# Down projections by Strassen–Winograd products on pairs of row blocks, with the first two row blocks of each half computed by themselves from the same operands

## The chip, the cores and the metric

One core of a Trainium2 chip runs the whole program. The metric is the device time of one execution in microseconds (us). TensorE (PE) does the matmuls and loads their weights on a second track (PEld), VectorE (DVE), ScalarE (ACT) and GpSimd (POOL) work on the data in SBUF and PSUM, and SyncE (SP) issues the loads of the weights.

## The reference

Two layers, an S5 mixer and a differential attention, each followed by a gated MLP with a convolution of width 3. The change concerns the last line of `conv_ffn`, the product with `w_down`.

```python
D_MODEL, SEQ, D_FF = 1024, 512, 2816

def conv_ffn(h, w_up, conv_w, conv_b, w_down):
    u = h @ w_up
    ...
    g, val = jnp.split(u, 2, axis=-1)
    return (jax.nn.silu(g) * val) @ w_down

def reference(x, ...):
    h = x
    for i in range(DEPTH):
        hn = rmsnorm(h, norm_mix_g[i])
        ...
        h = h + conv_ffn(rmsnorm(h, norm_ffn_g[i]), ffn_w_up[i], ...)
    return rmsnorm(h, final_norm_g)
```

## The kernel before

Everything is held transposed: 128 features on the partitions, 512 positions along a row. `h` has 8 row blocks (1024 features), the hidden layer of the MLP has 22 (2816).

**Numbers.** A float32 operand is split into hi (rounded to fp32r by an ACT copy) and lo (the rest, by a DVE subtraction). A product of two 128-blocks is three matmuls, hi by hi, hi by lo and lo by hi (`mm3`, L801 to L804). The third of them is the first that needs the lo of the weights.

**Weights.** `WStream` (L112 to L150) brings one unit after another from DRAM into `raw` (two buffers, transfers issued by SP) and splits it into hi (L139, ACT) and lo (L141, DVE, a few by POOL). A unit of an up projection has 2048 columns, split in halves of 1024. A unit of a down projection has 1408 columns, 11 blocks of 128 for one row block of the result, split in a first part of 640 columns (blocks k = 0 to 4) and a second part of 768 (k = 5 to 10). The hi and lo tiles have two buffers of 2048 columns. The next unit is split while the present one is multiplied.

**The MLP** (`ffn`, L909). `up(j)` computes for the hidden block j the two groups gv = 0 (gate) and gv = 1 (value) of 24 matmuls of 512 columns. When a group ends, `evac` (L918) multiplies it by the norm on DVE (`tpb`, L927) and `conv` (L933) runs one group later: two STT (scalar_tensor_tensor) of the convolution (L934, L935), SiLU or the product of the two (L944), and the hi (ACT, L945) and lo (DVE, L946) of the result, which is an operand of the down projection. `up` runs for j = 0 to 11, `down(0)` takes blocks 0 to 10 (half 0), `up` runs for j = 12 to 21, `down(1)` takes blocks 11 to 21 (half 1). In `down` (L993), each row block m is one PSUM bank of 11 × 3 matmuls of 512 columns, added into `h[:, m]` on DVE (L1005). In half 1 the norm of the next stage is begun with each row block (`norm_part`, L815): a square on ACT, a sum into `ssum` on POOL (L829), in layer 0 also the hi and lo (`xlo`, L821) of the next stage's input. In layer 1 the last two row blocks are done by `finish` in halves of 256 columns.

**Order.** Each engine runs its instructions in the order in which the program is written out; a semaphore holds an instruction back until what it reads is there. The second part of a unit's lo, and what `conv` leaves behind, are written out behind the `tpb` of the last group, so at the start of `down` DVE still has that queue to work through.

Stages, by the trace: S5 mixer and its gate to 211 us, layer 0 up 211 to 345, down half 0 to 407, up to 519, down half 1 to 581, attention to 859, layer 1 up to 993, down half 0 to 1055, up to 1167, down half 1 and the finish to the end.

Of the kernel before, what the change touches and what calls it, by code (L numbers as in the profile page):

```python
# [37 lines left out]
def trunk(ctx, tc, xs, xt, sp, bx, cx, sv, vec, lamv, biasw, wglu, wup, wdn, wv, wqk, wo, out):  # L38
# [72 lines left out]

    class WStream:  # L112
# [11 lines left out]

        def split(self, half, parts="hl", eng=V):

            i = self.ns
            if i >= len(units):
                return
            n = units[i][1]  # L130
            if half == 0 and "h" in parts:
                self.hl[i] = (
                    self.whl.tile([128, 2048], F32R, tag="hi", name=f"hi{i}"),
                    self.whl.tile([128, 2048], F32R, tag="lo", name=f"lo{i}"),
                )
            h0, h1 = (0, n // 256 * 128) if half == 0 else (n // 256 * 128, n)
            hi, lo = self.hl[i]
            if "h" in parts:
                S.activation(hi[:, h0:h1], self.raw[i][:, h0:h1], AF.Copy)  # L139
            if "l" in parts:  # L140
                eng.tensor_tensor(lo[:, h0:h1], self.raw[i][:, h0:h1], hi[:, h0:h1].bitcast(F32), op=ALU.subtract)  # L141
                if half == 1:
                    del self.raw[i]
                    self.ns += 1

        def start(self):
            self.cur += 1
            while self.nd < min(self.cur + 3, len(units)):
                self.dma()
            return self.hl.pop(self.cur)  # L150
# [573 lines left out]
    ws.whl = pool("whl", 2, "right")  # L724
# [71 lines left out]
    xhi = xnp.tile([128, 8, 512], F32R, name="xhi")  # L796
# [18 lines left out]
    def norm_part(m, gcol, first, split=True):  # L815

        settle()
        if split:
            gc = vect[:, gcol + m:gcol + m + 1]
            S.activation(xhi[:, m], h[:, m], AF.Copy, scale=gc)  # L820
            pend.append(lambda: V.scalar_tensor_tensor(  # L821
                xlo[:, m], h[:, m], gc, xhi[:, m].bitcast(F32), op0=ALU.mult, op1=ALU.subtract))
# [86 lines left out]
    def ffn(l, next_gcol):  # L909
        fp = pool(f"ffn{l}", 1, "left")  # L910
        tpb = [fp.tile([128, 514], F32, name=f"tpb{i}") for i in range(4)]
# [3 lines left out]
        acts = {}  # L915
        state = {"rb": None, "slot": None, "nt": 0}
# [4 lines left out]
        def evac(j, gv, ps):  # L921
            tb = tpb[state["nt"] % 4]
# [5 lines left out]
            acc = fp.tile([128, 512], F32, tag="acc", name="acc", bufs=4)  # L928
# [4 lines left out]
        def conv(j, gv, tb, cw, acc):  # L933
# [7 lines left out]
            if j % 4 == 0:  # L941
                state["slot"] = arena(F32R, [128, 4, 2, 512], f"act{l}_{j}")
            hi, lo = (state["slot"][:, j % 4, i] for i in range(2))
            V.tensor_tensor(a0, a0, acc, op=ALU.mult)  # L944
            S.activation(hi, a0, AF.Copy)  # L945
            later.append(lambda: V.tensor_tensor(lo, a0, hi.bitcast(F32), op=ALU.subtract))  # L946
            acts[j] = (hi, lo)
# [44 lines left out]

        def down(hf):  # L993
            flush()
            for m in range(8 if hf == 0 or l == 0 else 6):
# [5 lines left out]
                ps = psd[0].tile([128, 512], F32, tag="mm", name="ps", bufs=6)  # L1001
# [3 lines left out]
                V.tensor_tensor(h[:, m], ps, h[:, m], op=ALU.add)  # L1005
                if hf == 1 and l == 0:
                    norm_part(m, next_gcol, m == 0)
                elif hf == 1:
                    norm_part(m, next_gcol, m == 0, False)
                    S.activation(hg[:, m], h[:, m], AF.Copy, scale=vect[:, next_gcol + m:next_gcol + m + 1])  # L1010

        def finish():
# [36 lines left out]
            for c in range(2):  # L1049
                cs = slice(256 * c, 256 * c + 256)  # L1050
                for m in (6, 7):
# [7 lines left out]
                    ps = psd[0].tile([128, 512], F32, tag="mm", name="ps", bufs=6)[:, 0:256]  # L1059
                    for k in range(11):  # L1060
                        ah, al = acts[11 + k]
                        mm3(ps, wh[:, k * 128:k * 128 + 128], wl[:, k * 128:k * 128 + 128], ah[:, cs], al[:, cs],
                            k == 0, k == 10)
# [6 lines left out]
                    V.tensor_tensor(h[:, m, cs], ps, h[:, m, cs], op=ALU.add)  # L1070
# [11 lines left out]
        for j in range(12, 22):  # L1082
            up(j)
        down(1)
# [16 lines left out]
    for eh in range(2):  # L1101
        vps = [bank(t, "vps") for t in (("sc", "sc", "sc", "tr"), ("pj", "pj", "pv", "sc"))[eh]]
        for un in range(4):
            wh, wl = ws.start()
            ws.split(0)
            ws.split(1)
            for kl in range(2):
# [289 lines left out]
    fin = pool("fin", 1, "left")  # L1397
    hg = fin.tile([128, 8, 512], F32, name="hg")
# [4 lines left out]
    fin.release()  # L1403
# [108 lines left out]
```

## Time and profile before

| | us |
|---|---|
| median of 3 runs (1245.04 to 1246.16) | 1245.08 |
| the profiled execution | 1244.49 |
| its span, first to last instruction | 1242.7 |
| PE busy | 1181.4 (95%) |
| DVE busy | 826.3 (66%) |
| ACT busy | 583.3 (47%) |
| POOL busy | 253.1 (20%) |

The mean granted TensorE clock is 0.981. The page gives busy times and the chain of work that ended last. The timeline gives each instruction its start, its duration and, in brackets, the idle time of its engine before it and what ended that. Neighbouring instructions overlap in their records, so the spacing of starts is what an instruction takes of its engine in a row of like ones. In the windows view the granted clock is 1.00 at 2.4 GHz and 0.50 at 1.2 GHz.

### The profile page before, as it was taken

How to read it: one execution, taken by the hardware profiler on the slowest of the kernel's cores; microseconds unless marked ns; L12 is line 12 of the kernel's file. 1: busy time of each engine (PE TensorE's matmuls, PEld its weight loads, DVE VectorE, ACT ScalarE, POOL GpSimd, SP SyncE). 2: the span in 40 equal slices, each digit the busy share in tenths (PEclk: the TensorE clock that was granted, in tenths of full speed). 3: DMA queues.
4: the chain of work that ended last, by engine and by line, in shares of the span. 5: the costliest groups of instructions: out<-in, count | busy, mean ns of one | idle time of the engine just before them, and what ended most of it. 6: DMA issues, size and time to landing. Idle time of an engine off the chain costs nothing.

```text
span 1242.7 us, 16642 instructions
## 1 busy us (share of the span) xinstructions
PE 1181.4 (95%) x6402; PEld 933.9 (75%) x6402; DVE 826.3 (66%) x1654; ACT 583.3 (47%) x1008; POOL 253.1 (20%) x271
## 2 busy tenths in 40 slices
PE   3886899999999999999999999999999999999996
PEld 1663688888878888788876777678888878888786
DVE  8999866667653476744349899977767643566634
ACT  6775654444422344433247777655444421344431
POOL 3999424000000000011033434423000000000011
PEclk8998899999999999999999999999999999999998
DMA  5005323123233122132332323221222233122222
GB/s 219 2 3 136 137 74 104 66 102 102 81 102 109 69 98 102 70 117 71 98 107 83 90 75 108 70 76 63 96 77 94 81 117 125 68 96 75 92 94 68
DMA packets 23391, 112.32 MB, mean 90 GB/s; under 512 B 2704, under 2 KB 5392, under 8 KB 16144
## 3 DMA queue, kind: packets, MB, share of 16 engines
q1 hardware_dynamic: 21472, 108.64, 25.7%
q0 software_dynamic: 1280, 2.10, 0.9%
q8 instruction: 50, 0.82, 0.3%
q10 hardware_dynamic: 560, 0.52, 0.1%
q14 instruction: 29, 0.24, 0.1%
HBM read 102.86 MB, written 2.10 MB: 84 GB/s over the span
## 4 chain that ended last, share of the span: by engine, by line
PE 84%; DVE 5%; issue 1%; DMA 0%; ACT 0%; DVEq 0%; ACTq 0%
PE ps L803 20%; PE ps L804 20%; PE ps L802 20%; PE pj L802 2%; PE pj L804 2%; PE pj L803 2%; PE po L802 1%; PE po L803 1%; PE po L804 1%; PE vps L1112 1%; PE vps L1114 1%; PE vps L1113 1%; DVE qkt L1165 1%; PE ptp L1266 1%; PE sc L1231 1%; PE sc L1234 1%
## 5 line engine op out<-in xcount | busy, mean ns | idle before, releaser
L802 PE MATMUL ps<-xhi,hi 128*128 128x512 f32 x672 | 266.6, 397 | 0.0
L804 PE MATMUL ps<-xhi,lo 128*128 128x512 f32 x672 | 265.4, 395 | 0.0
L803 PE MATMUL ps<-xlo,hi 128*128 128x512 f32 x672 | 265.0, 394 | 0.0
L139 ACT ACTIVATE hi<-raw 128x1024 fp32r<-128x1024 f32 (+2 forms) x216 | 184.1, 874 | 113.6 <-PE ps L803 85.9
L141 DVE TENSOR_TENSOR lo<-raw,hi 128x1024 fp32r<-128x1024 f32 (+3 forms) x178 | 188.3, 1077 | 43.5 <-ACT hi L139 41.8
L927 DVE TENSOR_TENSOR tpb<-ps,rb 128x512 f32<-128x512 f32 x88 | 60.8, 693 | 149.7 <-PE ps L804 144.5
L929 ACT ACTIVATE acc<-tpb,vect 128x512 f32<-128x512 f32 x88 | 71.6, 816 | 168.1 <-DVE tpb L927 168.1
L804 PEld LDWEIGHTS ps<-xhi,lo 128*128 128x128 f32 x672 | 126.2, 188 | 31.1
L803 PEld LDWEIGHTS ps<-xlo,hi 128*128 128x128 f32 x672 | 126.2, 188 | 30.4
L802 PEld LDWEIGHTS ps<-xhi,hi 128*128 128x128 f32 x672 | 126.2, 188 | 30.0
L803 PE MATMUL ps<-act,hi 128*128 128x512 f32 (+1 forms) x374 | 143.2, 383 | 0.2
L802 PE MATMUL ps<-act,hi 128*128 128x512 f32 (+1 forms) x374 | 143.1, 383 | 0.0
L804 PE MATMUL ps<-act,lo 128*128 128x512 f32 (+1 forms) x374 | 142.9, 382 | 0.0
L827 POOL COPY ssum<-sqt 128x512 f32<-128x512 f32 x4 | 2.5, 626 | 656.2 <-ACT sqt L824 656.2
L1005 DVE TENSOR_TENSOR h<-ps,h 128x512 f32<-128x512 f32 x30 | 20.7, 691 | 107.5 <-PE ps L804 107.5
L141 POOL TENSOR_TENSOR lo<-raw,hi 128x512 fp32r<-128x512 f32 (+1 forms) x38 | 61.2, 1616 | 125.4 <-ACT hi L139 125.3
L803 PEld LDWEIGHTS ps<-act,hi 128*128 128x128 f32 x374 | 70.3, 188 | 16.0 <-DVE act L946 1.1
L804 PEld LDWEIGHTS ps<-act,lo 128*128 128x128 f32 x374 | 70.2, 188 | 16.1 <-DVE lo L141 1.4
L802 PEld LDWEIGHTS ps<-act,hi 128*128 128x128 f32 x374 | 70.3, 188 | 14.9
L935 DVE SCALAR_TENSOR_TENSOR acc<-tpb,vect,acc 128x512 f32<-128x512 f32 x88 | 66.2, 752 | 3.1
L934 DVE SCALAR_TENSOR_TENSOR acc<-tpb,vect,acc 128x512 f32<-128x512 f32 x88 | 65.5, 745 | 0.6 <-ACT acc L929 0.6
L945 ACT ACTIVATE act<-acc 128x512 fp32r<-128x512 f32 x44 | 27.9, 634 | 66.2 <-DVE acc L944 66.2
(262 smaller groups left out, 2048.7 us busy)
## 6 DMA issues: line engine op xcount, KB each, us to landing
raw<-wup SPq DMA_DIRECT2D x44, 1024.0 KB, 4.8
raw<-wdn SPq DMA_DIRECT2D x32, 704.0 KB, 4.0
raw<-wqk SPq DMA_DIRECT2D x16, 512.0 KB, 3.5
raw<-wglu SPq DMA_DIRECT2D x4, 1024.0 KB, 4.8
raw<-wv SPq DMA_DIRECT2D x8, 512.0 KB, 3.5
raw<-wo SPq DMA_DIRECT2D x4, 1024.0 KB, 4.9
bias<-biasw SPq DMA_DIRECT2D x8, 448.0 KB, 4.2
cxt<-cx SPq DMA_DIRECT2D x1, 2064.0 KB, 15.8
```

The costliest lines, as they stand in the source:

```text
L139: S.activation(hi[:, h0:h1], self.raw[i][:, h0:h1], AF.Copy)
L141: eng.tensor_tensor(lo[:, h0:h1], self.raw[i][:, h0:h1], hi[:, h0:h1].bitcast(F32), op=ALU.subtract)
L802: PE.matmul(ps, lhsT=wh, rhs=xh, start=first, stop=False)
L803: PE.matmul(ps, lhsT=wh, rhs=xl, start=False, stop=False)
L804: PE.matmul(ps, lhsT=wl, rhs=xh, start=False, stop=last)
L927: V.tensor_tensor(tb[:, 1:513], ps, state["rb"], op=ALU.mult)
L929: S.activation(acc, tb[:, 1:513], AF.Identity, bias=cb, scale=cw[1])
L934: V.scalar_tensor_tensor(acc, tb[:, 0:512], cw[0], acc, op0=ALU.mult, op1=ALU.add)
L935: V.scalar_tensor_tensor(acc, tb[:, 2:514], cw[2], acc, op0=ALU.mult, op1=ALU.add)
L945: S.activation(hi, a0, AF.Copy)
L1005: V.tensor_tensor(h[:, m], ps, h[:, m], op=ALU.add)
L1112: PE.matmul(vps[q], lhsT=xh, rhs=wk_h, start=(k == 0), stop=False)
```

## The change

Row blocks 2 to 7 of each down projection are computed in pairs (m, m+1). For each kp = 0 to 4 the two row blocks, two hidden blocks (2kp and 2kp+1) and two halves of 256 positions make a 2 × 2 by 2 × 2 product of blocks, for which Winograd's form of Strassen's algorithm takes seven block products in place of eight. A pair has 7 × 5 × 3 matmuls of 256 columns, and 2 × 2 × 3 for the eleventh hidden block ("left"), 117 in all, where two row blocks before had 66 of 512. `finish` still does row blocks 6 and 7 of layer 1's second half, so there are 3 + 3 + 3 + 2 = 11 pairs.

The operands of the activations are 7 tiles of 256 columns (`Acts`): op 0 is made when the even hidden block is done (`first`), the other six when the odd one is (`second`, with four DVE sums of 256 columns, and a lo of 1024 columns one group later). The weights' sums are made in `down` on DVE (`Pair.total`, 640 columns each), partly in the raw buffers themselves. In half 1, kp = 0 is put off by one group. A tile's hi and lo come from a pool of four buffers of 1024 columns, and a raw buffer's next transfer is issued where its last reader is written out, not in `start`. `tpb` and `acc` have three buffers in place of four, and `xlo` of row blocks 2 to 7 in layer 0 is made in the stage after. Rows 0 and 1 use the same operands: the even hidden blocks' first halves go to a bank `p1` (15 matmuls of 256 columns), then the odd blocks (15 of 512), then 15 of 256 with the difference (op 3), then left (3 of 512): 30 of 256 and 18 of 512 where there were 33 of 512.

```diff
+    class Pair:
...
+        def total(self, n):
+            w = self.view
+            if n == 2:
+                V.tensor_tensor(w(1), w(1, 0), w(1, 1), op=ALU.add)
+            elif n == 3:
+                V.tensor_tensor(w(1), w(1), w(0, 0), op=ALU.subtract)
+            elif n == 4:
+                self.x = self.ws.xtile().rearrange("p (n k c) -> p n k c", n=2, c=128)
+                V.tensor_tensor(self.x[:, 0], w(0, 1), w(1), op=ALU.subtract)
+            else:
+                V.tensor_tensor(self.x[:, 1], w(0, 0), w(1, 0), op=ALU.subtract)
...
+        def done(self, r):
+            del self.ws.raw[self.i + r]
+            self.ws.dma()
...
+        def tiles(self):
+            return [self.whl.tile([128, 1024], F32R, tag=t, name=t) for t in ("hi", "lo")]
...
-    ws.whl = pool("whl", 2, "right")
+    ws.whl = pool("whl", 4, "right")
...
+            wait = hf == 1 and kp == 0
+            if wait and jl % 2 == 1:
+                later.append(lambda: (ab.first(pa), later.append(lambda: ab.second(pa))))
+            elif not wait:
+                later.append(lambda: (ab.first if jl % 2 == 0 else ab.second)(pa))
...
+            def second(self, pa):
...
+                S.activation(self.hl[:, 0, 1:3], b[:, 1], AF.Copy)
+                V.tensor_tensor(x[:, 0], b[:, 0, 1], b[:, 0, 0], op=ALU.subtract)
+                V.tensor_tensor(x[:, 1], b[:, 1, 1], b[:, 0, 1], op=ALU.subtract)
+                V.tensor_tensor(x[:, 2], x[:, 1], b[:, 0, 0], op=ALU.add)
+                V.tensor_tensor(x[:, 3], b[:, 1, 0], x[:, 2], op=ALU.subtract)
+                S.activation(self.hl[:, 0, 3:7], x, AF.Copy)
+                V.tensor_tensor(self.hl[:, 1, 1:3], b[:, 1], self.hl[:, 0, 1:3].bitcast(F32), op=ALU.subtract)
...
         def down(hf):
...
+            for m in range(2):
                 wh, wl = ws.start()
                 if m == 0:
                     flush()
                 ws.split(0)
                 ws.split(1)
...
-                for k in range(11):
-                    ah, al = acts[hf * 11 + k]
-                    mm3(ps, wh[:, k * 128:k * 128 + 128], wl[:, k * 128:k * 128 + 128], ah, al, k == 0, k == 10)
...
+                for kp in range(5):
+                    block(p1[:, half[0]], 2 * kp, acts[hf, kp].op(0), kp == 0)
+                for kp in range(5):
+                    block(ps, 2 * kp + 1, [acts[hf, kp].hl[:, i, 1:3].rearrange("p n c -> p (n c)") for i in range(2)],
+                          kp == 0)
+                add(both(m), twice(p1[:, half[0]]))
+                for kp in range(5):
+                    block(ps[:, half[1]], 2 * kp, acts[hf, kp].op(3))
+                block(ps, 10, acts[hf, "left"])
...
+                prod(0, 0, "b1", 0, True)
+                if prev:
+                    prev()
+                w.l(2)
+                w.total(3)
+                w.h(3)
...
+                prod(5, 6, "b4", 0, True)
+                left(5, "b4")
+                add(h[:, m], bank["b2"])
+                norm(m)
+                ws.split(0, "l")
+                ws.split(1, "h")
+
+                prod(6, 4, "b1")
+                add(h[:, m + 1], bank["b4"])
+                ws.split(1, "l")
...
```

The first place is PE at the start of `down(0)` in layer 0. Before, the blocks come in the order k = 0, 1, 2, ..., and the rows shown are those of k = 4 and k = 5 (`act_4` holds hidden blocks 4 to 7).

```order
L802 MATMUL ps<-act_4_3006,hi_3407 128x512
L803 MATMUL ps<-act_4_3006,hi_3407 128x512
L804 MATMUL ps<-act_4_3006,lo_3408 128x512
L802 MATMUL ps<-act_4_3006,hi_3407 128x512 [waits Activation_49]
L803 MATMUL ps<-act_4_3006,hi_3407 128x512
L804 MATMUL ps<-act_4_3006,lo_3408 128x512 [waits DVE_49]
```

The block k = 5, with the waits on the second part of the weights, is there the sixth of the unit, and its third matmul the eighteenth. After, `act_0_3` is the operand tile of kp = 3, whose even hidden block is k = 6:

```order
L887 MATMUL ps<-xhi,lo 128x512
L1137 MATMUL ps<-act_0_0_2761,hi 128x256 [waits Activation_49]
L1137 MATMUL ps<-act_0_0_2761,hi 128x256
L1137 MATMUL ps<-act_0_0_2761,lo 128x256 [waits DVE_49]
L1137 MATMUL ps<-act_0_1_2918,hi 128x256 x2
L1137 MATMUL ps<-act_0_1_2918,lo 128x256
L1137 MATMUL ps<-act_0_2_3075,hi 128x256 x2
L1137 MATMUL ps<-act_0_2_3075,lo 128x256
L1137 MATMUL ps<-act_0_3_3232,hi 128x256 [waits Activation_49]
L1137 MATMUL ps<-act_0_3_3232,hi 128x256
L1137 MATMUL ps<-act_0_3_3232,lo 128x256 [waits DVE_49]
```

The waits on the second part have moved to the fourth block, and its third matmul is the twelfth of 256 columns.

The second place is DVE at the start of `down(1)` in layer 0, from the `tpb` of the last up group to the second part of the down unit's lo. Before:

```order
L927 TENSOR_TENSOR tpb_2586<-ps,rb 128x512 [waits PE_49]
L946 TENSOR_TENSOR act_20_4506<-acc,act_20_4506 128x512 [waits Activation_49]
L934 SCALAR_TENSOR_TENSOR acc<-tpb_2585,vect,acc 128x512
L935 SCALAR_TENSOR_TENSOR acc<-tpb_2585,vect,acc 128x512 [waits DVE_49]
L141 TENSOR_TENSOR lo_4474<-raw_4399,hi_4473 128x768 [waits Activation_49]
```

After, with the four sums of `second` (`x`) and the lo of the odd block (`fifth`, the tile of kp = 4):

```order
L1019 TENSOR_TENSOR tpb_2596<-ps,rb 128x512 [waits PE_49]
L1079 TENSOR_TENSOR x<-pa 128x256
L1080 TENSOR_TENSOR x<-pa 128x256 [waits DVE_49]
L1081 TENSOR_TENSOR x<-x,pa 128x256 [waits DVE_49]
L1082 TENSOR_TENSOR x<-pa,x 128x256 [waits DVE_49]
L1084 TENSOR_TENSOR fifth<-pa,fifth 128x512 [waits Activation_49]
L1026 SCALAR_TENSOR_TENSOR acc<-tpb_2595,vect,acc 128x512
L1027 SCALAR_TENSOR_TENSOR acc<-tpb_2595,vect,acc 128x512 [waits DVE_49]
L222 TENSOR_TENSOR lo<-raw_4806,hi 128x768
```

Four instructions of 256 columns have come in ahead of the 768 columns; at the start of `down(0)` the count there is as before.

The third place is DVE within `down(1)` of layer 0, over about half of a pair: the additions into `h`, the weights' sums (into `raw` and `x`), their lo, all written out between the products. Before, one row block was this:

```order
L1005 TENSOR_TENSOR h<-ps,h 128x512 [waits PE_49]
L821 SCALAR_TENSOR_TENSOR xlo<-h,vect,xhi 128x512 [waits DVE_49]
L141 TENSOR_TENSOR lo_4648<-raw_4597,hi_4647 128x640 [waits DMAHW1_49,Activation_49]
L141 TENSOR_TENSOR lo_4648<-raw_4597,hi_4647 128x768 [waits Activation_49]
```

After, from the addition of a pair's first row block on, into the next pair:

```order
L1148 TENSOR_TENSOR h<-ps,h 128x512 [waits PE_49]
L174 TENSOR_TENSOR lo<-raw_5160,hi 128x640 [waits Activation_49]
L177 TENSOR_TENSOR lo<-raw_5160,hi 128x128 [waits Activation_49]
L154 TENSOR_TENSOR raw_5204<-raw_5204 128x640 [waits DMAHW3_49]
L1148 TENSOR_TENSOR h<-ps,h 128x512 [waits DVE_49,PE_49]
L174 TENSOR_TENSOR lo<-raw_5204,hi 128x640 [waits Activation_49]
L156 TENSOR_TENSOR raw_5204<-raw_5204,raw_5160 128x640 [waits DVE_49]
L1148 TENSOR_TENSOR h<-ps,h 128x256 [waits PE_49]
L159 TENSOR_TENSOR x<-raw_5160,raw_5204 128x640 [waits DVE_49]
L161 TENSOR_TENSOR x<-raw_5160,raw_5204 128x640
L174 TENSOR_TENSOR lo<-raw_5204,hi 128x640 [waits Activation_49]
```

A pair has 11 such instructions of 640 columns on DVE, where two row blocks before had two of 640 and two of 768.

## Rows read from the trace of the kernel before

**Rows 1.** The page: busy time of PE, the chain by engine, landing of down weights.
```profile
PE 1181.4 (95%) x6402; PEld 933.9 (75%) x6402; DVE 826.3 (66%) x1654; ACT 583.3 (47%) x1008; POOL 253.1 (20%) x271
PE 84%; DVE 5%; issue 1%; DMA 0%; ACT 0%; DVEq 0%; ACTq 0%
raw<-wdn SPq DMA_DIRECT2D x32, 704.0 KB, 4.0
```

**Rows 2.** Timeline, PE, late down: start, us, engine, line, operation, operands, shape, count, [idle].
```profile
1194.63 0.40 PE L803 MATMUL ps<-act,hi 128*128 128x512 f32 x1
...
1213.07 0.39 PE L804 MATMUL ps<-act,lo 128*128 128x512 f32 x1
1213.30 0.28 PE L802 MATMUL ps<-act,hi 128*128 128x256 f32 x1
...
1220.37 0.28 PE L804 MATMUL ps<-act,lo 128*128 128x256 f32 x1
```

**Rows 3.** Timeline, start of down half 0, layer 0: PE, DVE and PEld.
```profile
345.06 0.40 PE L802 MATMUL ps<-act,hi 128*128 128x512 f32 x1
...
345.26 0.69 DVE L927 TENSOR_TENSOR tpb<-ps,rb 128x512 f32<-128x512 f32 x1 [1.93 <-PE ps L804]
345.86 0.68 DVE L946 TENSOR_TENSOR act<-acc,act 128x512 fp32r<-128x512 f32 x1
...
347.92 0.95 DVE L141 TENSOR_TENSOR lo<-raw,hi 128x768 fp32r<-128x768 f32 x1
...
348.92 0.19 PEld L804 LDWEIGHTS ps<-act,lo 128*128 128x128 f32 x1 [0.17 <-DVE lo L141]
```

**Rows 4.** Timeline, DVE and PEld in an odd up block's second group.
```profile
289.26 0.69 DVE L927 TENSOR_TENSOR tpb<-ps,rb 128x512 f32<-128x512 f32 x1 [1.53 <-PE ps L804]
...
291.92 1.22 DVE L141 TENSOR_TENSOR lo<-raw,hi 128x1024 fp32r<-128x1024 f32 x1
...
289.30 0.19 PEld L804 LDWEIGHTS ps<-xhi,lo 128*128 128x128 f32 x1
```

**Rows 5.** Timeline, DVE, early S5 stage: dependent steps of 256 columns.
```profile
17.14 0.41 DVE L296 TENSOR_TENSOR tsc<-tsc,PIh 128x256 f32<-128x256 f32 x1
17.48 0.19 DVE L345 TENSOR_SCALAR tsc<-tsc 128x64 f32<-128x64 f32 x1
17.58 0.42 DVE L298 TENSOR_TENSOR tsc<-tsc,PIh 128x256 f32<-128x256 f32 x1
```

**Rows 6.** Timeline, PEld, end of the first row block, down half 1.
```profile
526.36 0.19 PEld L803 LDWEIGHTS ps<-act,hi 128*128 128x128 f32 x1 [0.53 <-DVE act L946]
```

**Rows 7.** Groups by form (busy us, mean ns), 356:420; then DVE and POOL in half 1.
```profile
L141 DVE TENSOR_TENSOR lo<-raw,hi 128x640 fp32r<-128x640 f32 x5 | 4.1, 815 | 0.0
...
537.46 1.47 DVE L141 TENSOR_TENSOR lo<-raw,hi 128x640 fp32r<-128x640 f32 x1 [1.28 <-ACT hi L139]
...
536.94 1.30 POOL L829 TENSOR_TENSOR ssum<-ssum,sqt 128x512 f32<-128x512 f32 x1 [6.40 <-ACT sqt L824]
```

**Rows 8.** PE timeline after two idle stretches; windows: us, busy by engine, clock, DMA.
```profile
662.92 0.63 PE L1266 MATMUL ptp<-ident,s 128*128 128x128 f32 x4 [1.72 <-DVE mx L1250]
...
664.09 0.63 PE L804 MATMUL pj<-xhi,lo 128*128 128x512 f32 x1
...
666.65 0.55 PE L804 MATMUL pj<-xhi,lo 128*128 128x512 f32 x1
...
663.00:664.00 1.00, 1.00 (x6) 0.91 (x7) 1.00 (x2) 0.00 (x0) 0.91 (x1) 0.78 0.00 0
666.00:667.00 1.00, 1.00 (x4) 0.79 (x3) 1.00 (x2) 0.90 (x4) 0.00 (x0) 0.51 0.92 361
...
149.22 0.64 PE L747 MATMUL yf<-W,IZ 128*32 128x128 f32 x2 [3.63 <-ACT IZ L660]
...
154.00:156.00 2.00, 2.00 (x55) 1.80 (x47) 0.25 (x1) 1.26 (x2) 1.80 (x1) 0.76 0.03 8
```

**Rows 9.** The line that first reads h in the gate stage.
```profile
L898 DVE SCALAR_TENSOR_TENSOR h<-th,h x8: 691/692/693, 172.9 to 210.6; 128x512 f32<-128x512 f32 x8
```

More of the change, by code (lines that the diff above doesn't have):

```diff
@@ L130, in split @@
             n = units[i][1]
+            pair = i in pair_at
             if half == 0 and "h" in parts:
[L132 to L135, printed above, removed]
+                self.hl[i] = Pair(self, i) if pair else (Cols(), Cols())
+            if pair:
+                for c in parts:
+                    (self.hl[i].h if c == "h" else self.hl[i].l)(half)
+                if half == 1 and "l" in parts:
+                    self.ns += 2
+                return
             h0, h1 = (0, n // 256 * 128) if half == 0 else (n // 256 * 128, n)
@@ L138, in split @@
             if "h" in parts:
+                if half == 0 or n > 1024:
+                    for c, t in zip((hi, lo), self.tiles()):
+                        c.parts.append((t, h0, h1 if n > 1024 else n))
                 S.activation(hi[:, h0:h1], self.raw[i][:, h0:h1], AF.Copy)
@@ L813, in settle, with norm_part @@
         pend.clear()
-    def norm_part(m, gcol, first, split=True):
+    xlows = {}
+    def norm_part(m, gcol, first, split=True, put=None):
         settle()
@@ L909, in ffn @@
     def ffn(l, next_gcol):
+        hg = None
         fp = pool(f"ffn{l}", 1, "left")
-        tpb = [fp.tile([128, 514], F32, name=f"tpb{i}") for i in range(4)]
+        tpb = [fp.tile([128, 514], F32, name=f"tpb{i}") for i in range(3)]
         for t in tpb:
@@ L940, in conv @@
             a0 = state["gate"]
[L941 to L947, printed above, removed]
+            hf, jl = j // 11, j % 11
+            if jl == 10:
+                hi, lo = acts[hf, "left"] = [acts[hf, i].rest for i in range(2)]
+                V.tensor_tensor(a0, a0, acc, op=ALU.mult)
+                S.activation(hi, a0, AF.Copy)
+                later.append(lambda: V.tensor_tensor(lo, a0, hi.bitcast(F32), op=ALU.subtract))
+                return
@@ L991, in up, with mm2, twice, add @@
                     ws.split(gv, "l")
+        def mm2(ps, wh, wl, ah, al, first):
+            for i, (w, x) in enumerate(((wh, ah), (wh, al), (wl, ah))):
+                PE.matmul(ps, lhsT=w, rhs=x, start=first and i == 0, stop=True, skip_group_check=True)
         def down(hf):
             flush()
-            for m in range(8 if hf == 0 or l == 0 else 6):
+            half = (slice(0, 256), slice(256, 512))
+            def twice(x):
+                return x.unsqueeze(1).to_broadcast([128, 2, 256])
+            def add(dst, src):
+                V.tensor_tensor(dst, src, dst, op=ALU.add)
+            def both(r):
+                return h[:, r].rearrange("p (n c) -> p n c", c=256)
+            def norm(r):
+                if hf == 1 and l == 0:
+                    norm_part(r, next_gcol, r == 0, True, xlows if r > 1 else None)
+                elif hf == 1:
+                    norm_part(r, next_gcol, r == 0, False)
+                    S.activation(hg[:, r], h[:, r], AF.Copy, scale=vect[:, next_gcol + r:next_gcol + r + 1])
+            for m in range(2):
                 wh, wl = ws.start()
@@ L1000, in down @@
                 ws.split(1)
-                ps = psd[0].tile([128, 512], F32, tag="mm", name="ps", bufs=6)
-                for k in range(11):
-                    ah, al = acts[hf * 11 + k]
-                    mm3(ps, wh[:, k * 128:k * 128 + 128], wl[:, k * 128:k * 128 + 128], ah, al, k == 0, k == 10)
[L1005 to L1010, printed above, removed]
+                p1, ps = (psd[0].tile([128, 512], F32, tag="mm", name="ps", bufs=6) for _ in range(2))
@@ new lines, in block @@
+                def block(dst, k, x, first=False):
+                    mm2(dst, wh[:, 128 * k:128 * k + 128], wl[:, 128 * k:128 * k + 128], *x, first)
+                for kp in range(5):
[4 more added lines that the diff above has]
+                add(both(m), twice(p1[:, half[0]]))
@@ L1106, in trunk @@
             ws.split(1)
+            for k in (2 * un + 2, 2 * un + 3):
+                if k in xlows:
+                    xlows.pop(k)()
             for kl in range(2):
```

168 lines of the change are left out of this document (151 added, 17 removed).

## The prediction

> **What bounds the kernel now.** I read the page first, then the timeline of PE in the down stages, then what DVE and PEld do at their edges. PE is busy for 95% of the span and makes up 84% of the chain that ended last [rows 1], so a matmul that goes brings its time back, and a wait of PE is paid in full. In the middle of a down projection a matmul of 512 columns follows the next at (1213.07 − 1194.63) / 79 = 0.2333 us, and in the finish one of 256 at (1220.37 − 1213.30) / 59 = 0.1198 us [rows 2]. So half the columns cost a little more than half. The reader should then look at the edge between up and down: DVE writes the lo of the second weight part at the very end of its queue, and PE's weight load waits 0.17 us for it [rows 3]. What covers that queue before is the time that PE needs for the first blocks.
>
> **Matmuls.** A pair had 66 × 0.2333 = 15.40 us and gets 117 × 0.1198 = 14.02, a gain of 1.38. Eleven pairs give −15.2. Rows 0 and 1 go from 33 × 0.2333 = 7.70 to 30 × 0.1198 + 18 × 0.2333 = 7.79, +0.09; eight of them (two in each of four halves) give +0.75. This is the whole possible gain, 14.5 us.
>
> **The start of a down half, half 0.** PE starts at 345.06; the lo of columns 640 to 1407 starts on DVE at 347.92 and takes 0.95, so it is there at 348.87, and the weight load that needs it runs at 348.92 [rows 3]. Before, that is the eighteenth matmul of 512, at 17 × 0.2333 = 3.97 us, 349.03: a wait of almost nothing. After, PE takes the even blocks first, 256 columns each, and the twelfth matmul needs it, at 11 × 0.1198 = 1.32 us, 346.38. On DVE nothing goes ahead of it that was not there before. PE gets it at about 349.02 and stands 2.64 us, in both layers. There is no other matmul that could go first, since PE takes its instructions in order.
>
> **The same place, half 1.** Four sums of 256 columns now stand between the `tpb` and that lo. A step that needs the one before it takes 17.58 − 17.14 = 0.44 us, with one that doesn't 17.48 − 17.14 = 0.34 [rows 5], so 3 × 0.44 + 0.34 = 1.65: the lo starts 4.31 us after the `tpb` in place of 347.92 − 345.26 = 2.66, and PE stands 2.64 + 1.65 = 4.29 us. Together 2 × 2.64 + 2 × 4.29 = +13.9. Bounds: if the sums run without a wait (0.34 each) it is 13.3; if ACT's copy of the sums delays the queue by a step or so of 0.6, 15.
>
> What goes at the same place: PEld waited 0.53 us for the lo of the last hidden block (DVE act) [rows 6], of which PE lost 0.26. That block is now used last. −0.5 for two layers.
>
> **The clock after such a gap.** PE waited 1.72 us before 662.92. The granted clock was 0.78 in 663 to 664 and 0.51 in 666 to 667, so the lower level, 1.2 GHz, held from about 663.56 to 666.98, 3.42 us; matmuls of 512 columns stood (666.65 − 664.09) / 6 = 0.427 us apart there, against 0.233. That loses 0.45 of each us, 1.55 us. After the gap of 3.63 us before 149.22 the clock was still 0.76 over 154 to 156, so the lower level lasted until some 154.96, 5.74 us after PE resumed, 2.6 us lost [rows 8]. Gaps of 2.64 and 4.29 us lie on either side of the second: I take 1.55 for the short ones and 2.6 for the long ones, +8.3. Bounds: 0, if PE's work just before the gap keeps the clock up, and 4 × 2.6 = 10.4.
>
> **Up stages.** In an odd hidden block's second group DVE has 1.65 us of sums ahead of the lo of 1024 columns, which started 291.92 − 289.26 = 2.66 after its `tpb` and takes 1.22: it ends at 2.66 + 1.65 + 1.22 = 5.53. PE's load of that lo stood 0.04 behind the `tpb` [rows 4] and comes round 24 × 0.2333 = 5.60 later, so it fits by about 0.1 us. I take 0; 18 occurrences at 0.2 would be 3.6. The put-off block has the product (0.69 like a `tpb` [rows 3]) in the same queue, and ends 0.7 late: +1.4 for two layers. What covers these sums is DVE's idle time, which ended in a wait for PE of 1.53 us [rows 4]; it is used up here.
>
> **DVE within a pair.** By durations a pair has 11 instructions of 640 columns (0.815 [rows 7]), four additions of 512 (0.69 [rows 3]) and small ones, about 1.3 us in all, 13.0 of 14.02 us. Walked in the written order, with 0.74 us from one 640-column start to the next and 0.10 more for a dependent step, the addition of b4 begins at 12.42 us of the pair, 15.6 is reached before the next pair's first lo, and the lo of product 3 ends 5.9 us into that pair. PE wants it behind 51 matmuls and the two ahead of it, at 53 × 0.1198 = 6.35. So half 0 holds with 0.35 us to spare: 0.
>
> In half 1 POOL adds a square to `ssum` for each row. Where that ran beside DVE, 536.94 to 538.24, the lo of 640 columns took 1.47 instead of 0.815 [rows 7]: 0.65 lost in 0.78 us of overlap. For the two adds of a pair I take 0.8 for the first and 0.5 for the second, part of which falls on additions that read PSUM. A first pair sees one, 0.8 − 0.35 = 0.45; a later one both, 0.95. Two halves: 0.45 × 2 + 0.95 × 3 = +3.8. Bounds: 0, if they fall on idle time, and all eight adds at 1.30 less five times 0.3, 8.9.
>
> The Trainium skill (SBUF — State Buffer, "Who interferes with whom") says that a DVE instruction with two SBUF inputs contends with a GpSimd instruction that reads SBUF, while one with a single SBUF input does not. By that, an overlapped us would cost a whole us rather than 0.65 / 0.78, and the term above would be about 4.5; the trace agrees in kind and shows the smaller price.
>
> **What is hidden.** Raw transfers start earlier at some places; one takes 4.0 us to land [rows 1], and walked against the pair's need the nearest has 1 us to spare. The third gate-weight transfer now goes ahead of the loads of h on SP's queue; h is first read at 172.9 [rows 9], well behind. Attention keeps its order: 0, give or take 1.
>
> **Sum.** −15.2 + 0.75 + 13.9 − 0.5 + 8.3 + 1.4 + 3.8 = +12.4, against the profiled execution of 1244.49: 1256.9. The median of the runs lies 0.6 above that execution, so 1257.5.
>
> **Rivals.** *The stalls stay, the clock does not fall.* For it: PE is dense for long right up to the gap, which it was not ahead of either gap of [rows 8]. Against: the gap of 1.72 us was enough once [rows 8]. 12.4 − 8.3 gives 1249.2, still slower.
>
> *Only the stalls cost.* If the clock, POOL and the put-off block cost nothing, −15.2 + 0.75 + 13.9 − 0.5 = −1.1: 1244.0, no change.
>
> *The second weight part is there in time.* If DVE did the lo of 768 columns before PE needs it (a path that I see in no row; the order speaks against it), −14.5 − 0.5 and the later terms 0 to 5.2 give 1230 to 1235: faster. The mechanism is cover: it decides from the point at which the lo ends within 1.3 us of PE's start.
>
> *DVE becomes the bound in every pair.* Its slack of 0.35 us against 22 instructions goes at 0.016 us each. With 1.2 us more a pair, as the dependent steps and the waits for ACT's hi could bring, six pairs of half 0 lose about 0.85 and five of half 1 about 0.85 to 1.2 more: some +7 to +11, 1264 to 1268. This is the slower end.
>
> **How the numbers follow.** Forecast 0.62 (1251 to 1263, by the clock's and POOL's bounds), clock stays up 0.14, DVE bound 0.10, only the stalls 0.08, weights in time 0.06. The range goes from 1247, which takes in the second case, to 1264, where the slower one begins; that leaves out the two low cases and most of the high one. A measurement tells about 0.2% from no change, 2.5 us here. Slower: 0.62 + 0.10 + most of 0.14 less the forecast's low tail, 0.80. Same: 0.08 and the rest, 0.13. Faster: 0.07.
>
> **What would show it.** In the trace of after, PE idle of 2.6 us some 1.3 us behind the start of each `down(0)` and of 4.3 us in each `down(1)`, ended by the lo of the second weight part on DVE; granted clock 0.50 for 3 to 6 us behind each; seven products of 14.0 us per pair without a wait in half 0, and waits of under 1 us for DVE in half 1. I would be wrong if PE shows no idle there (then it is faster by over 1%), or if the pairs of half 0 wait for DVE (then slower than 1264).

## The result, and the profile after

The changed kernel takes 1253.31 us (median of 4 runs, 1251.83 to 1254.63) against 1245.06 of the kernel before (4 runs): a ratio of 1.0068, 95% interval 1.0054 to 1.0082. It is slower, by 8.2 us, where 12.4 were forecast. The profiled execution took 1252.57 us, its span is 1250.8 us, and its mean granted clock 0.974 (0.981 before).

The page of the kernel after, busy times and chain, as [rows 1]:

```profile
PE 1176.5 (94%) x7083; PEld 964.1 (77%) x7083; DVE 964.2 (77%) x1909; ACT 623.3 (50%) x1083; POOL 255.3 (20%) x269
PE 80%; DVE 16%; ACT 2%; issue 1%; DMA 0%; SPq 0%; DVEq 0%; ACTq 0%
```

PE is busy for only 4.9 us less, and DVE for 138 us more. In the view of waits (engine, line, what it waited for; us in total, times, longest) a group is new on PE:

```profile
PE ps L1137 <- DVE lo L222: 12.7, 4, 4.0
```

L1137 is the line of the matmuls of the down projections, and L222 makes the lo of weights that are split as a whole unit. The four waits are at the starts of the four down halves. The first of them, in the timelines of PE and DVE, is the place of [rows 3]:

```profile
345.12 0.40 PE L1137 MATMUL ps<-act,hi 128*128 128x256 f32 x2
347.91 0.39 PE L1137 MATMUL ps<-act,lo 128*128 128x256 f32 x1 [2.38 <-DVE lo L222]
...
346.90 0.95 DVE L222 TENSOR_TENSOR lo<-raw,hi 128x768 fp32r<-128x768 f32 x1
```

The half begins at 344.05. The two matmuls with the hi of block k = 6 run at once, and the third stands until the lo of 768 columns is there. In half 1 the same place has the four sums ahead of that lo:

```profile
519.33 0.40 PE L1137 MATMUL ps<-act,hi 128*128 128x256 f32 x2
523.70 0.58 PE L1137 MATMUL ps<-act,lo 128*128 128x256 f32 x1 [3.97 <-DVE lo L222]
...
518.45 0.69 DVE L1019 TENSOR_TENSOR tpb<-ps,rb 128x512 f32<-128x512 f32 x1 [1.93 <-PE ps L887]
519.06 0.41 DVE L1079 TENSOR_TENSOR x<-pa 128x256 f32<-128x256 f32 x1
519.39 0.42 DVE L1080 TENSOR_TENSOR x<-pa 128x256 f32<-128x256 f32 x1
519.84 0.42 DVE L1081 TENSOR_TENSOR x<-x,pa 128x256 f32<-128x256 f32 x1
520.30 0.42 DVE L1082 TENSOR_TENSOR x<-pa,x 128x256 f32<-128x256 f32 x1
...
522.70 0.95 DVE L222 TENSOR_TENSOR lo<-raw,hi 128x768 fp32r<-128x768 f32 x1
```

By the spacing of PE's starts, less what the matmuls take, the gaps cost 2.55 us in half 0 and 4.13 in half 1, and the same in layer 1. The third of them ends like the first:

```profile
1001.71 0.39 PE L1137 MATMUL ps<-act,lo 128*128 128x256 f32 x1 [2.38 <-DVE lo L222]
```

The clock, in the windows view of PE (window, length, busy time and count, granted clock, DMA share and GB/s), behind the four gaps:

```profile
348.00:349.00 1.00, 1.00 (x6) 0.78 0.17 51
349.00:351.00 2.00, 2.00 (x7) 0.50 0.94 315
351.00:352.00 1.00, 1.00 (x4) 0.51 0.10 39
352.00:354.00 2.00, 2.00 (x13) 1.00 0.65 214
522.00:523.00 1.00, 0.00 (x0) 0.82 0.00 0
524.00:528.00 4.00, 4.00 (x12) 0.50 0.56 182
529.00:530.00 1.00, 1.00 (x5) 0.76 0.00 0
...
1002.00:1004.00 2.00, 2.00 (x12) 1.00 0.62 158
...
1176.00:1180.00 4.00, 4.00 (x12) 0.50 0.56 180
```

It fell behind the gap of layer 0's half 0 for 3.4 us (348.6 to 352.0). In half 1 it fell already while PE stood (522.6) and stayed down until 529.5, and in layer 1's half 1 it did the same. Behind the gap of layer 1's half 0 it did not fall at all.

The table gives the time of each stage, worked out from the start of the first matmul of one to that of the next, and in the last row to the span's end. The wait at the start of the V stage thus stands in the row of layer 0's half 1. The runs in the last three columns are told below.

| stage, us | before | after | e3_fill | e1_lo_early | e9_weights_first |
|---|---|---|---|---|---|
| start to layer 0's up | 208.87 | 207.86 | 207.92 | 209.86 | 209.01 |
| down half 0, layer 0 | 61.81 | 61.72 | 60.17 | 57.54 | 57.54 |
| up, second part | 112.00 | 112.48 | 112.48 | 112.48 | 112.00 |
| down half 1, layer 0 | 61.96 | 66.93 | 64.32 | 62.21 | 59.05 |
| V to output projection | 275.91 | 276.49 | 275.21 | 276.00 | 276.43 |
| down half 0, layer 1 | 61.80 | 60.18 | 60.19 | 57.54 | 57.54 |
| up, second part | 112.00 | 112.48 | 112.48 | 112.48 | 112.18 |
| down half 1, layer 1, finish | 75.98 | 80.29 | 77.37 | 77.22 | 73.98 |

The two first parts of up, 136.2 us each, are the same in all.

### The profile page after: what moved, and what is told of

Same layout as the page of the kernel before. It is cut to its first block, busy times and chain, and to the rows that moved or that the text cites. A ratio compares the mean times of both kernels' runs of the same rounds, so it can differ in the third digit from the quotient of the medians.

```text
span 1250.8 us, 18479 instructions
## 1 busy us (share of the span) xinstructions
PE 1176.5 (94%) x7083; PEld 964.1 (77%) x7083; DVE 964.2 (77%) x1909; ACT 623.3 (50%) x1083; POOL 255.3 (20%) x269
## 4 chain that ended last, share of the span: by engine, by line
PE 80%; DVE 16%; ACT 2%; issue 1%; DMA 0%; SPq 0%; DVEq 0%; ACTq 0%
PE ps L1137 17%; PE ps L885 14%; PE ps L887 13%; PE ps L886 13%; DVE scn L773 2%; PE pj L885 2%; PE pj L887 2%; PE pj L886 2%; DVE St L779 1%; DVE acc L776 1%; PE po L885 1%; PE po L886 1%; PE po L887 1%; PE vps L1376 1%; DVE qkt L1429 1%; PE vps L1377 1%
## 5 line engine op out<-in xcount | busy, mean ns | idle before, releaser
L1137 PE MATMUL ps<-act,hi 128*128 128x256 f32 (+1 forms) x968 | 193.7, 297 | 0.0
L220 ACT ACTIVATE hi<-raw 128x1024 fp32r<-128x1024 f32 (+3 forms) x172 | 152.1, 898 | 26.7 <-DMA raw<-wv 9.5
L222 DVE TENSOR_TENSOR lo<-raw,hi 128x1024 fp32r<-128x1024 f32 (+3 forms) x134 | 147.5, 1111 | 15.8 <-ACT hi L220 14.0
L1137 PEld LDWEIGHTS ps<-act,hi 128*128 128x128 f32 x968 | 154.0, 191 | 4.8
L1137 PE MATMUL ps<-act,lo 128*128 128x256 f32 (+1 forms) x484 | 143.5, 296 | 13.8 <-DVE lo L222 12.7
L1137 PEld LDWEIGHTS ps<-act,lo 128*128 128x128 f32 x484 | 93.6, 193 | 18.0 <-DVE lo L222 13.5
L222 POOL TENSOR_TENSOR lo<-raw,hi 128x512 fp32r<-128x512 f32 (+1 forms) x38 | 60.8, 1605 | 125.6 <-ACT hi L220 125.5
L168 ACT ACTIVATE hi<-raw 128x640 fp32r<-128x640 f32 x55 | 40.0, 735 | 85.8 <-PE ps L1137 36.4
L1148 DVE TENSOR_TENSOR h<-ps,h 128x256 f32<-128x256 f32 (+1 forms) x82 | 50.5, 616 | 40.2 <-PE ps L1137 40.2
L918 POOL TENSOR_TENSOR ssum<-ssum,sqt 128x512 f32<-128x512 f32 x26 | 39.5, 1518 | 95.6 <-ACT sqt L913 95.5
L1029 ACT ACTIVATE acc<-acc 128x512 f32<-128x512 f32 x44 | 27.9, 633 | 60.4 <-DVE acc L1027 60.3
```

Source lines behind the costliest of these rows:

```text
L168: S.activation(hi[:, 0:640].rearrange("p (k c) -> p k c", c=128), self.src(n), AF.Copy)
L1137: PE.matmul(ps, lhsT=w, rhs=x, start=first and i == 0, stop=True, skip_group_check=True)
L1148: V.tensor_tensor(dst, src, dst, op=ALU.add)
```

## The experiments

The theory is the forecast's: the products on pairs give what the matmul count says, and the waits at the four starts, with the clock behind them, take more than that. The rivals are that DVE is simply too full, so that a wait removed comes back elsewhere, and that the clock or POOL has no part in it. Every ratio is to the kernel before.

**e1_lo_early: the lo ahead of the last group's `tpb`.**

```diff
-                evac(j, gv, ps)
-                if j > 1 or gv == 1:
-                    ws.split(gv, "l")
+                early = gv == 1 and j in (11, 21)
+                if early:
+                    ws.split(gv, "l")
+                evac(j, gv, ps)
+                if (j > 1 or gv == 1) and not early:
+                    ws.split(gv, "l")
```

> The changed kernel with one line moved: in the last up block before each down half, the lo of the second weight part is written out ahead of the tpb of the last group, into DVE's idle time there, in place of behind the convolution. Theory (the wait for this lo at the start of each half, and the lower clock behind it, take back the gain): in half 0 the two idle stretches of 2.4 us and the one clock fall go, -2 x 2.55 - 1.55 = -6.7; in half 1 the weights are there, and PE next waits for the lo of the last hidden block, about 2 us in place of 4.1, with or without a fall of the clock: -4.2 to -9.4 for two layers. In all 1237 to 1242.5. Rival (PE's wait is only the visible end of a DVE queue that is too long for both row blocks): the waits come back at the second row block, and the time stays above 1248.

1238.04 us, ratio 0.9948 (0.9929 to 0.9967). One lo, moved at each of the four starts, is worth 15 us and turns the change from slower to faster. Half 0 takes 57.54 us in both layers, without a wait. (The lo itself waited 0.7 us for ACT's hi and pushed the last `tpb` back by 0.8 us; PE lost nothing by it.) What is left in half 1, on PE:

```profile
524.69 0.49 PE L1140 MATMUL ps<-act,hi 128*128 128x512 f32 x1 [1.39 <-ACT act L1038]
525.42 0.50 PE L1140 MATMUL ps<-act,hi 128*128 128x512 f32 x1 [0.23 <-DVE act L1039]
```

That is the last hidden block, whose hi and lo come at the end of DVE's queue: the second wait that the expectation named. In the kernel after it did not show, since DVE had made up that work while PE stood at the first gap. Layer 1's half 1 had a fall of the clock (3.4 us) behind it, layer 0's had none.

**e2_pe_order: DVE as it is, PE asks later.**

```diff
-                for kp in range(5):
-                    block(p1[:, half[0]], 2 * kp, acts[hf, kp].op(0), kp == 0)
...
+                if m == 0:
+                    even(range(3))
+                    odd(range(2))
+                    diff(range(3))
+                    even(range(3, 5))
+                    odd(range(2, 5))
+                    add(both(m), twice(p1[:, half[0]]))
+                    diff(range(3, 5))
```

> The changed kernel with only PE's order in row block 0 altered: all work on blocks k = 0 to 4 first (3 x 3 of 256, 2 x 3 of 512, 3 x 3 of 256), then k = 5 to 10. DVE's order is as in the changed kernel. Theory: the second weight part is then needed 3.8 us after the start in place of 1.3, so the wait goes in half 0 (-2 x 2.55 - 1.55) and falls to about 1.7 in half 1, behind which the last hidden block's lo brings another 1 us: -1.4 each and perhaps no clock fall, -2.6 each. In all 1238 to 1244. Rival (DVE's queue is what counts, not when PE asks): the same time lost later in the half, 1250 or more.

1237.45 us, ratio 0.9942 (0.9926 to 0.9959), just under the range expected. This moves the other end of the same wait, with the same result. The view of waits has two of 1.5 us for the lo of 768 columns, both in half 1, and 0.7 us in each half 1 for the last hidden block.

```profile
PE ps L1137 <- DVE lo L222: 3.0, 2, 1.5
...
PE ps L1137 <- ACT act L1038: 1.0, 2, 0.5
...
PE ps L1137 <- DVE act L1039: 0.5, 2, 0.2
```

So it is neither the length of DVE's queue alone nor PE's order alone: the new order of the blocks spent the time that had covered DVE's queue. This was the step of the forecast on which all else rested.

**e3_fill: the gaps filled with matmuls that nothing reads.**

```diff
                 for kp in range(5):
+                    if m == 0 and kp == 3:
+                        spare = psd[0].tile([128, 512], F32, tag="mm", name="spare", bufs=6)
+                        o = acts[hf, 0].hl[:, 0, 1:3].rearrange("p n c -> p (n c)")
+                        for i in range(10 if hf == 0 else 17):
+                            PE.matmul(spare, lhsT=wh[:, 0:128], rhs=o, start=True, stop=True)
                     block(p1[:, half[0]], 2 * kp, acts[hf, kp].op(0), kp == 0)
```

> The changed kernel with spare matmuls of 512 columns into a PSUM bank that nothing reads, in the four gaps: 10 ahead of the wait in half 0, 17 in half 1 (2.33 and 3.97 us, a little less than the gaps). Nothing else changes and all of the computation is done. Theory (the clock falls because PE stands still): the granted clock stays at 1.00 through the four starts, the wait for the lo ends at the same time as before, and the time falls by the clock's part alone, 1.55 + 2 x 2.6 = 6.8 us: about 1246.5. Rival (the clock falls on its own there, or the cost attributed to it is the wait's): no change, 1253, or above it by what the spare matmuls overrun.

1244.19 us (10 runs), ratio 1.0002 (0.9992 to 1.0011), where about 1246.5 were expected. The wait ends when it ended before (3.86 us into half 0), and the clock stays up. These are windows of PE over both gaps of layer 0 and what follows:

```profile
346.00:348.00 2.00, 1.95 (x11) 1.00 0.00 0
348.00:352.00 4.00, 4.00 (x19) 1.00 0.56 180
519.00:523.00 4.00, 4.00 (x20) 1.00 0.00 0
523.00:527.00 4.00, 4.00 (x22) 1.00 0.57 180
```

The stages are shorter by 1.55, 2.61, 0 (layer 1's half 0 had no fall to lose) and 2.92: 7.1 us, against 6.8 expected. The rest of the 9.1 us between the medians is 1.3 in the attention, where this run had one stretch at 1.2 GHz of 3.4 us and the kernel after one of 6.8, and the spread of runs.

**e4_no_pool_adds: without POOL's additions in half 1's pairs.** The kernel leaves out the squares of row blocks 2 to 7 (2 to 5 in layer 1) from the norms' sum; those of rows 0 and 1 stay.

```diff
-        else:
+        elif count:
             G.tensor_tensor(ssum[0], ssum[0], sqt, op=ALU.add)
```

> The changed kernel without POOL's additions of the squares of row blocks 2 to 7 into ssum in the second down halves (rows 2 to 5 in layer 1); the norms that use the sum are thereby of fewer rows. Theory (POOL's additions slow DVE's weight sums, and PE waits for the lo of product 3): the waits of 0.27 to 0.63 us in the pairs of half 1 go, two of 0.63 and one of 0.27 in layer 0 and about 0.65 in layer 1, -2.2; the wait of 1 us at the start of the V stage stays. 1251. Rival (DVE's own queue in half 1 is too long): no change, 1253.

1250.70 us, 2.6 below the kernel after. The waits of the later pairs are gone. The 0.27 us of layer 0's first pair stay, contrary to the expectation, since row 1's addition, which meets that pair, was left in. In the kernel after, POOL, DVE and PE in the second pair read:

```profile
557.95 1.60 POOL L918 TENSOR_TENSOR ssum<-ssum,sqt 128x512 f32<-128x512 f32 x1 [3.76 <-ACT sqt L913]
...
557.57 0.82 DVE L156 TENSOR_TENSOR raw<-raw,raw 128x640 f32<-128x640 f32 x1
...
558.64 1.59 DVE L159 TENSOR_TENSOR x<-raw,raw 128x640 f32<-128x640 f32 x1
560.16 0.81 DVE L161 TENSOR_TENSOR x<-raw,raw 128x640 f32<-128x640 f32 x1
560.89 0.81 DVE L174 TENSOR_TENSOR lo<-raw,hi 128x640 fp32r<-128x640 f32 x1
...
561.76 0.39 PE L1137 MATMUL ps<-act,lo 128*128 128x256 f32 x1 [0.36 <-DVE lo L174]
```

Without the addition the sum at 558.64 takes 0.82:

```profile
558.18 0.82 DVE L159 TENSOR_TENSOR x<-raw,raw 128x640 f32<-128x640 f32 x1
```

The other addition of a pair, at the end of the first in the kernel after, meets the lo of 640 columns for its last 0.28 us, and that takes 0.97:

```profile
552.90 1.29 POOL L918 TENSOR_TENSOR ssum<-ssum,sqt 128x512 f32<-128x512 f32 x1 [7.95 <-ACT sqt L913]
...
553.91 0.97 DVE L174 TENSOR_TENSOR lo<-raw,hi 128x640 fp32r<-128x640 f32 x1
```

The two second halves are shorter by 1.27 and 0.83 us, 2.1 against 2.2 expected. The wait of 0.88 us at the V stage stays. That the whole time fell by about as much is in part luck: the attention was 1.1 us shorter, and layer 1's half 0 was 1.5 longer, by a fall of the clock that the kernel after has not.

**e6_no_pairs: all row blocks computed like rows 0 and 1.**

```diff
+    pair_at = set()
...
-            for m in range(2):
+            for m in range(8 if hf == 0 or l == 0 else 6):
...
-            for m in (2, 4, 6) if hf == 0 or l == 0 else (2, 4):
+            for m in ():
```

> The changed kernel with the products on pairs undone: all row blocks are computed as rows 0 and 1 are (30 matmuls of 256 columns and 18 of 512 each, from the same operands, without weight sums), everything else as in the changed kernel. Theory (the products on pairs give what the matmul count says, and all that the change loses lies in the operands and the start of a half): + 11 x (15.58 - 14.02) = +17.2, less the waits for product 3, -2.2: about 1268. Rival (the pairs give less, since DVE is loaded with 13 of 14 us): 1260 or less.

1265.45 us, 12.1 above the kernel after, where 15 were expected: nearer the theory than the rival. Layer 0's half 0, with the same wait and clock fall in both, is 66.43 against 61.72: 4.71 for three pairs, 1.57 each, the count's 1.56. Half 1 of layer 0 is longer by only 1.07, since it has no waits for product 3 and none at V (0.27 + 0.63 + 0.63 + 1.04), and a fall of the clock of 3.4 us in place of 6.8, worth 1.05. Of the 3 us that the expectation missed, 1.04 are the wait at V, 1.05 this fall, 1.2 a shorter attention (275.33 us for 276.49), 0.5 a shorter start and 0.7 layer 1's half 1; against them stands 1.5 in layer 1's half 0, where the clock fell in this run and not in the kernel after. So the pairs do bring what they promise, and half 1 gives part of it back.

**e5_all: every wait of the trace taken away by order.** On top of e1_lo_early: in half 1, row block 1's weights ahead of the last hidden block's product, and that block's matmuls of row 0 within row block 1; the put-off up block's lo early; product 3's lo ahead of the sum for product 6; the V stage's PSUM banks swapped.

```diff
-                w.total(6)
                 w.l(3)
+                w.total(6)
                 w.done(0)
...
+                if m == 0 and hf == 1:
+                    def rest(ps=ps, block=block):
+                        block(ps, 10, acts[hf, "left"])
+                        add(h[:, 0], ps)
+                        norm(0)
+                    first_left.append(rest)
+                    continue
```

> The changed kernel with each wait that its trace shows taken away by order alone, all of the computation done: the lo of the second weight part ahead of the last tpb (as in the run on that); in half 1 the lo of row block 1's weights ahead of the last hidden block's product, and the three matmuls of row block 0 with that block moved into row block 1's time; in the put-off up block the lo of the next weights ahead of its tpb; in each pair the lo of product 3 ahead of the sum for product 6; at the V stage the PSUM banks of its two halves swapped. Theory: against 1238.0 of the first of these steps alone, -3.8 (two waits of 1.9), -1.0 (two up blocks), -1.7 (product 3 in half 1), -1.0 (V) and -1.5 where the clock no longer falls: about 1229, 1227 to 1232. Rival (the queue of DVE in half 1 is full, and the waits come back at other places): 1234 or more.

1234.86 us, ratio 0.9915 (0.9898 to 0.9932): above what the theory said, at the rival's bound. The up blocks (112.00) and the wait at V came out as expected. The waits for product 3 in layer 0 grew to 1.35, 0.94 and 1.32 us (the expectations of e7_base and e9_weights_first leave out the 0.1 us that the matmul behind each loses). In the two later pairs ACT waited 3.3 and 3.6 us for a transfer, here the second:

```profile
558.13 0.74 ACT L168 ACTIVATE hi<-raw 128x640 fp32r<-128x640 f32 x1 [3.64 <-DMA raw<-wdn]
```

The sum for product 6 is the last reader of the first raw buffer. In the trace it ends at 553.64, SP issues the next transfer at 553.70, and that lands at 558.02. Put behind a lo of 0.74 us, the sum lets this transfer start that much later.

**e7_base: that step undone.**

```diff
-                w.l(3)
                 w.total(6)
+                w.l(3)
                 w.done(0)
```

> The kernel of the run e5_all with one of its steps undone: in each pair the lo of product 3 stands behind the sum for product 6 again, as in the changed kernel; all of the computation is done. Theory (that step released the first raw buffer 0.74 us later, and the next pair's weights then came in late: ACT waited 3.3 to 3.6 us for their transfer): the waits for product 3 in half 1 of layer 0 fall from 0.84 and 1.21 us to the 0.6 of the changed kernel, and the time by 1 to 2 us, to 1233 to 1234. Rival (these waits come from POOL's additions and DVE's full queue alone, whatever the order): 1235 as in e5_all, or more.

1237.07 us, ratio 0.9938 (0.9924 to 0.9951), slower than e5_all and not faster. The later pairs did what was expected, 0.70 and 0.62 us for 0.94 and 1.32. But the first pair of each half 1 got worse, 2.09 for 1.35 in layer 0, and layer 1 had a fall of the clock behind it. The 0.74 us between the two are the sum for product 6, which stands ahead of the lo of product 3 again. The larger part of that wait is older; DVE in this run and in e5_all:

```profile
529.05 0.83 DVE L174 TENSOR_TENSOR lo<-raw,hi 128x640 fp32r<-128x640 f32 x1 [1.94 <-ACT hi L168]
...
530.79 0.82 DVE L174 TENSOR_TENSOR lo<-raw,hi 128x640 fp32r<-128x640 f32 x1 [1.94 <-ACT hi L168]
```

In both, ACT did the norm's work on row 0 ahead of these weights.

**e8_late_squares: the squares of layer 0 moved into the V stage**, on top of e7_base.

```diff
+            for f in sums:
+                f()
+            sums.clear()
```

> The kernel of the run e7_base, with the squares of row blocks 2 to 7 of layer 0's second down half and POOL's additions of them moved behind the pairs, to the first unit of the V stage, and the norm's statistics one unit later; all of the computation is done. Theory (POOL's additions slow DVE within the pairs, at a price of 0.3 to 0.7 us of PE each pair): the waits for product 3 in that half go, about -2 against e7_base, 1231 to 1232. Rival (the additions then slow DVE in the V stage as much): the same as e7_base.

1239.44 us, 2.4 above e7_base. The later pairs lost their waits, as without the additions, but the V stage got two of its own and a fall of the clock, and the stages to the output projection took 282.49 us for 276.82. The work came back at another place, as the rival said, and cost more there.

```profile
PE vps L1409 <- DVE v L1421: 2.6, 1, 2.6
PE vps L1411 <- DVE xlo L909: 1.8, 1, 1.8
```

**e9_weights_first: e7_base with the first pair's weights ahead of the norm of row 0.**

```diff
                 if first_left:
                     first_left.pop()()
-                    ws.split(1)
...
                         block(ps, 10, acts[hf, "left"])
+                        ws.split(1, "h")
                         add(h[:, 0], ps)
+                        ws.split(1, "l")
                         norm(0)
```

> The kernel of the run e7_base with one place reordered: in half 1 the hi and lo of the first pair's second weights stand ahead of the norm work of row block 0, which in e7_base ACT did first (DVE's lo waited 1.9 us for ACT there); all of the computation is done. Theory (the first pair's wait of 1.98 us in layer 0, and of 0.46 and 1.3 us in layer 1, comes from that order): these fall to about 0.5 each, -1.5 and -1.2, and the clock fall behind them in layer 1 goes, -1.5 in runs that have it: 1232.5 to 1234.5. Rival (DVE's work at the start of half 1 is too long in any order): 1236 to 1237.5 as before.

1232.26 us, ratio 0.9897 (0.9880 to 0.9913), 13 us below the kernel before and 21 below the change as it was. The first pair's wait in layer 0 is 0.27 us, and all that the view of waits still has for weights is this:

```profile
PE ps L1140 <- DVE lo L174: 1.1, 3, 0.4
```

These three are the later pairs, with POOL's additions, which stay. The time was 0.2 us below the range expected.

## Why the prediction was right, and where its terms were off

The direction and the mechanism held: the starts of the four halves took 13.4 us and the clock another 6.8, against 14.5 that the matmuls were to give. The size was 4.2 us too high. By the steps of the prediction:

- **Matmuls.** Half 0 without waits is 57.54 us, which is 2 × 7.79 + 3 × 13.99; a pair was put at 14.02. Against 61.80 that is −4.26, where −3.96 was reckoned: the old half was 0.2 us longer than eight times 7.70. Over the four halves that is some 0.8 us more gain than the sum had.
- **The starts.** 2.55 and 4.13 us for 2.64 and 4.29. The walk of DVE's queue, instruction by instruction, and the count of matmuls before the first that needs it were enough for that; e1_lo_early and e2_pe_order moved either end and got the time back. One price in it came out by luck. Of the two steps of [rows 5] that start 0.44 us apart, the second does not need the first (L298 reads nothing that L296 wrote), and between them ran the one at 17.48. The sums in the trace after do show the price: 0.45 and 0.46 us for the two that need the one before, 0.33 for the one that does not. The wait of [rows 6] is gone, but not for the reason given, that its block is now used last: without the first gap the same block waits longer (1.39 and 0.23 us in e1_lo_early).
- **The clock.** 6.8 us for 8.3. The long gaps cost 2.6 each by the price of [rows 8] (2.6 and 2.9 by e3_fill's stages); of the two short ones one cost 1.55 and the other nothing. The rival that the clock stays up was half right there, and only there. e3_fill shows that it is the standing still, not the stage, that brings the clock down.
- **Up stages.** The put-off block cost 0.48 us in place of 0.7, and the 18 others nothing, as taken.
- **DVE within a pair.** Half 0 held without a wait, on a slack that had been put at 0.35 us (6.35 − 5.9 is 0.45; in the trace, the lo ends at 383.67 and its matmul starts at 384.13). In half 1 the waits cost 0.27, 0.63 and 0.63 us in layer 0 and 0.66 in layer 1, 2.2 in all for 3.8. The price of the first addition was right (0.77 us lost at 558.64, put at 0.8). The other addition of the pair cost DVE only 0.15 us (at 553.91), where 0.5 was put. Both reach the path to product 3: its lo ends 8.40 us behind the addition of b4 (553.30) in half 1 and 7.48 behind the same one (376.19) in half 0, 0.92 us more, of which the slack takes half. The share of 0.65 / 0.78 was no rate: overlaps of 0.78, 0.91 and 0.28 us cost DVE 0.65, 0.77 and 0.15, each time the whole overlap less 0.13 or 0.14. By the rule of the Trainium skill cited in the prediction (SBUF — State Buffer, "Who interferes with whom"), a DVE instruction with two SBUF operands is the one that suffers, and that is what the trace shows: the additions that read PSUM kept their 0.69 and 0.42 us beside POOL. (In the rival with DVE as the bound, the lower end of +7 is 9.4 by its own figures, 11 × 0.85; that case did not come.)
- **Missed.** The V stage loses 1.04 us to a wait for the last addition, because its first PSUM bank is that of the last product. With the banks swapped (e5_all) the wait is gone. The prediction took the end of the half as free.
- **Start and attention.** They changed by −1.0 and +0.6 us, and were put at 0. Within the S5 stage, the stretch at 1.2 GHz of [rows 8] that lasts 6.8 us in the profile before lasts 3.4 in the one after, which by the same price is worth up to 1.55. It differs between the profiles here, with nothing changed at that place: the four with 3.4 us reach layer 0's up at 207.4 to 207.9, the others at 207.9 to 209.9. What sets it is not shown.

The terms that were sized too high (clock 1.5, DVE 1.6, waits 0.5, up 0.4), the larger gain of 0.8, and the start with the attention (0.4), less the 1.0 that was missed, make up the 4.2 us between 1257.5 and 1253.3. Nearly all of them err the same way.

## What to carry to other kernels

A change that shortens the work of the bounding engine also shortens the time that covers what another engine has queued at a stage's edge. Count, in the bounding engine's new order, when it first needs each late operand, and set that against the end of the other engine's queue. A wait of a few us there costs its length and, at three of the four places here, the lower clock behind it. Moving one instruction ahead of the edge, into time in which its engine mostly waits anyway, was worth 15 us, where the whole change had cost 8. Where an engine is at 13 of 14 us, reordering for one wait shows up at the next (a buffer released later, a norm ahead of weights), so take the trace after each step.

## What was not expected of the hardware

Two gaps of the same 2.38 us, at the same place in the program, differ: in layer 0 the clock fell 0.7 us after PE had resumed, in layer 1 it stayed at 1.00, and in e4_no_pool_adds, with the same gaps, it fell at both. Nor does the length alone decide: in e7_base it fell behind a gap of 1.19 us in layer 1 and not behind one of 1.82 in layer 0. In the gap of 3.97 us it fell 1 us before PE resumed, so part of the slow stretch cost nothing, and in e6_no_pairs, after the same gap in layer 0, 1 us after. What decides it stays open. Matmuls that nothing reads, put into the gaps, took 7.1 us off the four halves, nearly all that the change had lost, without any of the waits becoming shorter.

Between DVE and POOL it is the one that begins second that is slowed. In [rows 7] POOL's addition began first and took 1.30 us, as it does with no such DVE work beside it (1.29 at 1218.86 in the kernel after), and DVE lost the overlap. At 557.95 the addition took 1.60, because the sum of 557.57 was still running on DVE. The two overlap by 0.44 us, and POOL lost 0.30: again the overlap less 0.14, while that sum took its usual 0.82. DVE's sum at 558.64 began second and lost 0.77.
